# Keys' high and low parts written to the other half of the partitions by ACT copies in place of DMAs, in both mixers of a two-layer encoder step

## The chip, the cores and the metric

The kernel runs on one core of a Trainium2 chip. The engines are named as in the profile: PE is TensorE (PEld its weight loads), DVE VectorE, ACT ScalarE, POOL GpSimd, SP SyncE. PE multiplies, DVE and ACT do elementwise work; SP and POOL issue nearly all DMAs, each from a queue of its own that is worked off in order. The metric is the device time of one execution in microseconds (us), lower is better.

## The reference

One inference step over 1024 prompt frames and 8 running streams with 16 new frames each, so T = 1152 tokens of width 1024. Each of two layers is a mixer and an MLP, with RMS norms ahead. The two mixers, cut to what the change touches:

```python
def stick_breaking(q, k, v, q_pos, k_pos):          # layer 0: 8 heads of 64, beside a convolution
    z = jnp.einsum('bqhd,bkhd->bhqk', q, k).astype(jnp.float32) * (HEAD_DIM ** -0.5)
    mask = k_pos[None, :] < q_pos[:, None]
    log_keep = jnp.where(mask, jax.nn.log_sigmoid(-z), 0.0)
    between = lax.cumsum(log_keep, axis=3, reverse=True) - log_keep
    w = jnp.where(mask, jnp.exp(jax.nn.log_sigmoid(z) + between), 0.0)
    return jnp.einsum('bhqk,bkhd->bqhd', w.astype(v.dtype), v)

def band_attention(q, k, v, q_pos, k_pos, rel_bias):   # layer 1: 16 heads of 64
    s = jnp.einsum('bqhd,bkhd->bhqk', q, k).astype(jnp.float32) * (HEAD_DIM ** -0.5)
    rel = jnp.clip(q_pos[:, None] - k_pos[None, :], -REL_CLIP, REL_CLIP) + REL_CLIP
    s = s + rel_bias[:, rel].astype(jnp.float32)
    ...
    p = jax.nn.softmax(jnp.where(mask, s, -jnp.inf), axis=-1)
    return jnp.einsum('bhqk,bkhd->bqhd', p.astype(v.dtype), v)
```

In layer 1 a query sees its own chunk of 64 frames and the 8 chunks before it. The mixer's output is multiplied by an output matrix and added to the residual stream.

## The kernel before, in words

Products are taken in float32 by way of float32r, a format with fewer mantissa bits: a number is split into a high part (its float32r rounding, an ACT copy, line 185) and a low part (the rest, a DVE subtraction, line 186), and products of the parts are summed.

**Pairs of heads.** Both mixers go over pairs of heads: `mixer0` four (times 60 to 600 us), `mixer1` eight (1317 to 1930 us), some 70 us each in `mixer1`. A head has 64 dimensions, so a pair fills the 128 partitions: head 0 the lower half, head 1 the upper. While pair p is attended to, the projections of pair p+1 (`psc` in `mixer1`, `psp` in `mixer0`, with the split weights `hl_wc`, `hl_wi`) are worked off between its steps, into the buffers `sq`, `sk`, `sv` (queries, keys, values over 1152 tokens).

**`expand`** (line 342) then makes the operands of the scores for each head i of the pair, on 128 partitions: `qs[i]` has the scaled query's high part in the head's own half and its low part in the other half; `kd[i]` has the key's high part in both halves, `kl[i]` its low part in both halves. So one pass over 128 partitions gives (query high + query low) · key high, and a second one · key low. The profile writes these tiles as `q`, `k` and `l`. The own half of `kd` comes from ACT (line 348), that of `kl` from DVE (line 351); the other halves are copied from the own half by DMAs from POOL's queue (lines 349 and 352, 256 KB each).

**Scores and products.** PE multiplies into `z` (lines 943, 944) or `zc` (1220, 1221). In `mixer1`, DVE adds the bias and takes the maximum (1184), ACT exponentiates (`s`, 1187), DVE inverts the sum (1188) and normalises (1189); PE transposes the weights into `tpc` (457); ACT and DVE split them into `whc` and `wlc` (185, 186); PE multiplies with the values (`avc`, 469); ACT moves a half of the result (`atc`, 477), DVE adds it (`cpc`, 479) and POOL's queue stores it to `cat_d` in DRAM (363). In `mixer0` a sigmoid (`sg`, 947), a scan on DVE (928), transposes `tpa` (388), an ACT copy `wa` (390) and products `ava` (398) stand in the places of these.

**Output.** During the last pair the output product begins. `ready_chunks` loads the earlier pairs' results from `cat_d` into `cr` (1081, SP's queue) and splits them into `cat`, `part_out` loads the residual stream into `xo` (1098 in layer 0, 1100 in layer 1) and multiplies `cat` with the output weights into `psoa`. `cr` is a tile with the tag of the key buffer `sk`, and there is one such buffer, so a load of `cr` waits for whoever reads the keys last; `xo` has the tags of `sq` and `sv`, and its load waits for their last readers. `ct03k`, also on SP's queue, is the key cache of the samples.

**What sets the order.** The steps of a pair and the projections are merged by a list of costs in the program, and within that a scheduler places each instruction on its engine's queue by estimated readiness. Each engine works its queue in order. An instruction that takes another time, or another engine, can so move others on all engines.

```python
# ready_chunks
cr = pp.tile([P, T], F32, "sk", f"cr{layer}{c}")
dma(cr, cat_d[layer][c])
for g in range(NG):
    hi, lo = (x[:, c % 4, :] for x in cat_t[g][c // 4])
    split(hi, lo, cr[:, g * G:g * G + G])
```

Of the kernel before, what the change touches and what calls it, by code (L numbers as in the profile page):

```python
# [10 lines left out]
AF = mybir.ActivationFunctionType  # L11
# [8 lines left out]
TP = 1024  # L20
# [20 lines left out]
def f(ap):  # L41
    return ap.bitcast(F32)
# [82 lines left out]
def tile_trunk(ctx, tc, ins, outs):  # L125
    nc = tc.nc
    ACT = nc.scalar.activation
# [214 lines left out]
    def expand(qs, kd, kl, q, k):  # L342


        for i in range(2):
            own = slice(64 * i, 64 * i + 64)
            oth = slice(64 - 64 * i, 128 - 64 * i)
            ACT(kd[i][own], k[own, :TP], AF.Copy)
            nc.gpsimd.dma_start(kd[i][oth], kd[i][own])
            ACT(qs[i][own], q[own, :TP], AF.Copy, scale=0.125)  # L350
            tt(kl[i][own], k[own, :TP], f(kd[i][own]), ALU.subtract)
            nc.gpsimd.dma_start(kl[i][oth], kl[i][own])
            stt(qs[i][oth], q[own, :TP], 0.125, f(qs[i][own]), ALU.mult, ALU.subtract)

    class Cat:
# [301 lines left out]
    def mixer0():  # L657
        with ExitStack() as st:
# [228 lines left out]
            def expand_qk(p):  # L887
                q, k = S["sq", p], S["sk", p]
                expand(qs, kd, kl, q, k)
                S["qn"] = pp.tile([P, P], F32, "qn", f"qn0{p}")  # L890
                S["kn"] = pp.tile([P, P], F32, "kn", f"kn0{p}")
                ACT(S["qn"], q[:, TP:], AF.Copy, scale=0.125)
                ACT(S["kn"], k[:, TP:], AF.Copy)
# [222 lines left out]
    def mixer1(nx, win):  # L1116
        h, rstd = nx.h, nx.r
        with ExitStack() as st:
# [37 lines left out]
            def expand_qk(p):  # L1156
                q, k = S["sq", p], S["sk", p]
                expand(qs, kd, kl, q, k)
                S["qn"] = pp.tile([P, P], F32, "qn", f"qn1{p}")
                S["kn"] = pp.tile([P, P], F32, "kn", f"kn1{p}")  # L1160
                ACT(S["qn"], q[:, TP:], AF.Copy, scale=0.125)
                ACT(S["kn"], k[:, TP:], AF.Copy)
# [823 lines left out]
```

## Time and profile before

| | |
|---|---|
| three runs | 2727.28, 2727.0, 2727.28 us (median 2727.28) |
| the profiled execution | 2730.68 us, of which 2728.9 us from the first to the last instruction |
| granted clock of TensorE, mean | 0.993 |
| PE busy | 2662.6 us, 98% of the span |
| DVE, ACT, POOL busy | 2040.6, 1365.7, 330.5 us |
| DMA | 422.90 MB in 173203 packets |
| output product, `mixer0` and `mixer1` | from 400 us and from 1836 us on |

A row of the timeline reads: start in us, duration in us, engine, line, operation, what is written from what, shape, how many in a row, and in brackets how long the engine stood idle before it and what ended that. "128x512" is partitions by elements. A window's row reads: its ends, its length, busy time and number of instructions of PE, PEld, DVE, ACT and POOL, PE's granted clock (1 is full), the mean busy share of the DMA engines, GB/s. SPq and POOLq are the issuing queues.

### The profile page before, as it was taken

What the parts mean: (1) busy time and instruction counts of PE and PEld (TensorE: products, weight loads), DVE (VectorE), ACT (ScalarE), POOL (GpSimd) and SP (SyncE); (2) the same over time, 40 slices, a digit from 0 to 9 for tenths busy, and PEclk for the clock granted to TensorE, in tenths of its full rate; (3) what the DMA queues carried; (4) which work ended last, traced back from release to release, by engine and by line L of the source; (5) the groups of instructions that cost most, each with busy time, mean ns of one, the idle gap of its engine ahead of it and who ended that gap; (6) DMA issues with size and microseconds to landing.
All of it is one profiled execution on the core that took longest, in us unless ns stands there. A gap on an engine that the chain in (4) does not pass through costs nothing.

```text
span 2728.9 us, 50505 instructions
## 1 busy us (share of the span) xinstructions
PE 2662.6 (98%) x19362; PEld 2553.8 (94%) x19362; DVE 2040.6 (75%) x4105; ACT 1365.7 (50%) x2854; POOL 330.5 (12%) x599
## 2 busy tenths in 40 slices
PE   8999998999999999999999999998999999999998
PEld 8888886899999999999999999997999999999998
DVE  7999996787777755768577777778787777647577
ACT  5344456755555543445355555555455555534344
POOL 1000111131111100000011111110321111100001
PEclk9999999999999999999999999999999999999999
DMA  4344447443333486335444444446543334674344
GB/s 159 104 128 149 146 141 241 171 145 141 140 138 138 151 290 224 108 113 178 145 141 139 129 139 141 137 127 218 181 140 138 143 141 147 233 254 135 96 125 146
DMA packets 173203, 422.90 MB, mean 155 GB/s; under 512 B 25968, under 2 KB 53808, under 8 KB 170912
## 3 DMA queue, kind: packets, MB, share of 16 engines
q1 hardware_dynamic: 135696, 288.38, 32.6%
q0 software_dynamic: 37120, 131.27, 13.9%
q8 instruction: 152, 2.49, 0.4%
q14 instruction: 91, 0.75, 0.1%
q10 hardware_dynamic: 144, 0.02, 0.0%
HBM read 289.60 MB, written 117.34 MB: 149 GB/s over the span
## 4 chain that ended last, share of the span: by engine, by line
PE 84%; DVE 7%; ACT 3%; issue 3%; DMA 3%; POOL 0%; SPq 0%; DVEq 0%; ACTq 0%; POOLq 0%
PE pd L1705 26%; PE um L1480 25%; PE psc L225 10%; PE psp L225 4%; PE avc L469 2%; PE tpc L457 2%; PE psoa L225 2%; PE f L225 1%; PE zs L570 1%; PE zc L1220 1%; PE ava L398 1%; DVE y L737 1%; PE so L604 1%; PE psg L225 1%; PE psa L225 1%
## 5 line engine op out<-in xcount | busy, mean ns | idle before, releaser
L225 PE MATMUL psc<-h,hl_wc 128*128 128x384 f32 x1728 | 327.1, 339 | 0.0
L225 PEld LDWEIGHTS psc<-h,hl_wc 128*128 128x128 f32 x1728 | 296.8, 188 | 13.3 <-issue 10.9
L1480 PE MATMUL um<-sl,hl_m 128*128 128x288 f32 x1548 | 240.8, 296 | 0.0
L1480 PEld LDWEIGHTS um<-sl,hl_m 128*128 128x128 f32 x1548 | 218.2, 189 | 0.0
L1705 PE MATMUL pd<-tm,hl_wd 128*128 128x288 f32 x1584 | 214.7, 294 | 0.0
L1705 PEld LDWEIGHTS pd<-tm,hl_wd 128*128 128x128 f32 x1584 | 211.3, 189 | 0.0
L737 DVE SCALAR_TENSOR_TENSOR y<-u,dw,y 128x1024 f32<-128x1024 f32 (+1 forms) x232 | 177.5, 805 | 0.7
L1487 ACT ACTIVATE hdm<-hdm 128x288 f32<-128x288 f32 x192 | 84.7, 442 | 156.4 <-DVE hdm L1486 154.8
L225 PE MATMUL psp<-h,hl_wi 128*128 128x384 f32 x864 | 162.5, 340 | 0.0
L186 DVE TENSOR_TENSOR tm<-xr,tm 128x576 fp32r<-128x576 f32 (+1 forms) x120 | 85.7, 715 | 94.8 <-ACT tm L185 94.6
L225 PEld LDWEIGHTS psp<-h,hl_wi 128*128 128x128 f32 x864 | 148.4, 188 | 6.2 <-issue 5.1
L185 ACT ACTIVATE tm<-xr 128x576 fp32r<-128x576 f32 (+1 forms) x120 | 77.6, 647 | 94.7 <-PE pd L1705 75.9
L1480 PE MATMUL um<-sl,hl 128*128 128x288 f32 x756 | 119.1, 296 | 0.0
L1187 ACT ACTIVATE s<-s,mxc 128x640 f32<-128x640 f32 (+4 forms) x128 | 88.8, 694 | 60.2 <-DVE mxc L1184 58.6
L1705 PE MATMUL pd<-th,hl_wd 128*128 128x288 f32 x792 | 113.9, 297 | 3.8 <-DVE th L186 3.7
L1705 PEld LDWEIGHTS pd<-th,hl_wd 128*128 128x128 f32 x792 | 108.7, 191 | 4.5 <-DVE th L186 4.2
L1705 PE MATMUL pd<-xr,hl_wd 128*128 128x288 f32 x792 | 111.9, 295 | 0.0
L1705 PEld LDWEIGHTS pd<-xr,hl_wd 128*128 128x128 f32 x792 | 107.4, 189 | 0.0
L1480 PEld LDWEIGHTS um<-sl,hl 128*128 128x128 f32 x756 | 106.4, 188 | 0.8
L1705 PE MATMUL pd<-tm,hl 128*128 128x288 f32 x768 | 104.9, 295 | 0.0
L1705 PEld LDWEIGHTS pd<-tm,hl 128*128 128x128 f32 x768 | 103.1, 188 | 0.0
L185 ACT ACTIVATE whc<-tpc 128x512 fp32r<-128x512 f32 (+1 forms) x144 | 72.5, 523 | 46.7 <-PE tpc L457 45.7
(530 smaller groups left out, 6536.8 us busy)
## 6 DMA issues: line engine op xcount, KB each, us to landing
xr<-hb_d SPq DMA_DIRECT2D x208, 288.0 KB, 2.9
xr<-in_w_up_dram SPq DMA_DIRECT2D x64, 512.0 KB, 4.0
hb_d<-hdm POOLq DMA_DIRECT2D x96, 288.0 KB, 2.4
hb_d<-t POOLq DMA_DIRECT2D x96, 288.0 KB, 2.4
wm<-in_w_down_dram SPq DMA_DIRECT2D x64, 256.0 KB, 4.1
st_wd<-in_w_down_dram SPq DMA_DIRECT2D x64, 256.0 KB, 3.5
st_wc<-in_w_in_c_dram SPq DMA_DIRECT2D x44, 256.0 KB, 2.6
xm_d<-xo POOLq DMA_DIRECT2D x16, 576.0 KB, 3.8
```

The costliest lines, as they stand in the source:

```text
L185: ACT(hi, src, AF.Copy)
L186: return tt(lo, src, f(hi), ALU.subtract)
L225: mm(ps()[:, :G], hl[:, a, at:at + P], act[g][k // 4][b][:, k % 4, :], start=n == 0, stop=n == len(todo) - 1)
L398: mm(st["av"][64 * m:64 * m + 64, o0:o0 + n], vs[:, j, i], st["w"][gi][:, c0:c0 + n], start=gi == 0, stop=gi == last)
L457: nc.tensor.transpose(tp[:, c0 + q * P:c0 + (q + 1) * P], blocks.get(j, tile_q), ident)
L469: mm(st["av"][:, o0:o0 + n], vs[:, j, i].rearrange("p a d -> p (a d)"), src[:, c0:c0 + n], start=st["done"] == 0, stop=st["done"] == nmm - 1)
L570: mm(box["z"][at // 512][own, at % 512:at % 512 + kw], qb[:, own], k[:, b * kw:b * kw + kw], start=True, stop=True)
L737: stt(src if j == CW - 1 else dst, src, wj, dst, ALU.mult, ALU.add)
L1187: ACT(s[:, :n], s[:, :n], AF.Exp, bias=mx, scale=-1.0, accum_out=tot)
L1480: mm(banks[b, n][:, :TQ], w[:, a, c * P:c * P + P], combo(key, c)[:, h, n * TQ:n * TQ + TQ], start=k < 3 and c == 0 and i == 0, stop=c == ...
L1487: ACT(y, y, AF.Relu)
L1705: mm(ps, w[:, a, m * P:m * P + P], b[:, h, (n - ns[0]) * TQ:(n - ns[0]) * TQ + TQ], start=first and s == 0, stop=j == NJ - 1 and s == 2, s ...
```

## The change

In `expand`, the two DMAs are replaced by ACT copies. The key's other half is rounded from the keys again, which gives the same high part; the low part's other half is copied from DVE's result. The key copy stands after the query's.

```diff
             ACT(kd[i][own], k[own, :TP], AF.Copy)
-            nc.gpsimd.dma_start(kd[i][oth], kd[i][own])
             ACT(qs[i][own], q[own, :TP], AF.Copy, scale=0.125)
+            ACT(kd[i][oth], k[own, :TP], AF.Copy)
             tt(kl[i][own], k[own, :TP], f(kd[i][own]), ALU.subtract)
-            nc.gpsimd.dma_start(kl[i][oth], kl[i][own])
+            ACT(kl[i][oth], f(kl[i][own]), AF.Copy)
             stt(qs[i][oth], q[own, :TP], 0.125, f(qs[i][own]), ALU.mult, ALU.subtract)
```

In the changed program the copy of the query's high part is line 349, the key copy 350, the copy of the low part 352. Twelve pairs of two heads make 24 of each. The scheduler's order changes with it, and these are the places that matter below.

SP's queue at the last pair boundary of `mixer0`, between the loads of the key cache and of the output weights:

```order
 L539 DMA ct03k_4424<-in_sb_k_dram 128x4x256
 L539 DMA ct03k_4426<-in_sb_k_dram 128x4x256
+L1098 DMA xo_4607<-in_x_dram 128x3x384
 L1081 DMA cr_4356<-cat_d_109 128x1152
-L1098 DMA xo_4607<-in_x_dram 128x3x384
 L192 DMA st_wo0a_0_5016<-in_w_out_ab_dram 128x384
 L192 DMA st_wo0a_0_5182<-in_w_out_ab_dram 128x384
```

The load of the residual stream (`xo`) moved ahead of the load of an earlier pair's result (`cr`); `cr` waits for ACT now where it waited for DVE.

ACT at the same place (`sb` belongs to the samples, `sv` are the next values, `ata` is the moved half of a product):

```order
 L947 ACTIVATE sg_4252<-z_4257 128x512
 L608 ACTIVATE sb_4280<-so_4093 128x128
 L390 ACTIVATE wa_4286<-tpa_4282 128x384
+L350 ACTIVATE k_744<-sk_3769 64x1024
 L881 ACTIVATE sv_4091<-psp_4237 128x384
-L185 ACTIVATE hl_wo0a_0_4715<-st_wo0a_0_4713 128x384
-L902 ACTIVATE ve_4489<-sv_4091 64x8 x4
+L352 ACTIVATE l_746<-l_746 64x1024
 L411 ACTIVATE ata_4320<-ava_4313,ve_3530 64x128 x2
 L390 ACTIVATE wa_4371<-tpa_4366 128x512
```

The key copy, the last reader of the key buffer now, stands behind the first `wa`.

ACT at a steady boundary of `mixer1`, where pair 6's operands are made (the boundaries from pair 1 on look alike):

```order
 L348 ACTIVATE k_14069<-sk_19255 64x1024
 L185 ACTIVATE whc_19739<-tpc_19736 128x256
-L350 ACTIVATE q_14067<-sq_18957 64x1024
+L349 ACTIVATE q_14067<-sq_18957 64x1024
+L350 ACTIVATE k_14069<-sk_19255 64x1024
 L1187 ACTIVATE s_19721,totc_19732<-s_19721,mxc_19730 128x640
 L477 ACTIVATE atc_19751<-avc_19716 64x256
+L352 ACTIVATE l_14071<-l_14071 64x1024
 L185 ACTIVATE whc_19799<-tpc_19794 128x512
 L185 ACTIVATE whc_19821<-tpc_19816 128x512
```

The key copy stands ahead of the exponential, the low part's copy ahead of the next split.

DVE at the same boundary:

```order
 L351 TENSOR_TENSOR l_14071<-sk_19255,k_14069 64x1024
+L353 SCALAR_TENSOR_TENSOR q_14067<-sq_18957,q_14067 64x1024
 L1188 RECIPROCAL totc_19732<-totc_19732 128x1
 L479 TENSOR_TENSOR cpc_19753<-avc_19716,atc_19751 64x256
 L1189 TENSOR_SCALAR s_19721<-s_19721,totc_19732 128x640
-L353 SCALAR_TENSOR_TENSOR q_14067<-sq_18957,q_14067 64x1024
 L186 TENSOR_TENSOR wlc_19800<-tpc_19794,whc_19799 128x512
```

The query's low part moved ahead of the normalisation of the weights. On PE the six transposes of these weights moved behind seven matmuls of the next pair's projection.

ACT at the boundary of pairs 6 and 7 of `mixer1`, some instructions later:

```order
 L477 ACTIVATE atc_20646<-avc_20611 64x256
+L352 ACTIVATE l_14071<-l_14071 64x1024
 L185 ACTIVATE whc_20676<-tpc_20671 128x512
 L185 ACTIVATE whc_20695<-tpc_20690 128x512
+L185 ACTIVATE cat_00_20682<-cr_20680 128x384 x3
 L185 ACTIVATE whc_20727<-tpc_20724 128x256
-L185 ACTIVATE cat_00_20682<-cr_20680 128x384 x3
+L185 ACTIVATE vs_14072<-vt_20760 128x6x64
```

The three splits of `cr` stand ahead of the last `whc` of pair 6. On PE three transposes of the values (`vt`) moved ahead of the product with that `whc`.

## The prediction

> **What bounds the kernel now.** I read first the page's busy shares and its chain by engine, then the waits of TensorE, then single stretches of the two mixers.
>
> ```profile
> PE 2662.6 (98%) x19362; PEld 2553.8 (94%) x19362; DVE 2040.6 (75%) x4105; ACT 1365.7 (50%) x2854; POOL 330.5 (12%) x599
> PE 84%; DVE 7%; ACT 3%; issue 3%; DMA 3%; POOL 0%; SPq 0%; DVEq 0%; ACTq 0%; POOLq 0%
> ```
>
> TensorE (PE) is busy for 98% of the span, ACT for half of it. So ACT has room for more work on average, and the question is only where TensorE stands waiting and whether the new copies lie ahead of what it waits for. The waits of PE (us in total, times, longest), four rows of that view:
>
> ```profile
> PE psoa L225 <- ACT cat L185: 8.0, 3, 5.7
> PE avc L469 <- ACT whc L185: 6.9, 7, 1.1
> PE tpc L457 <- DVE s L1189: 6.1, 8, 3.2
> PE avc L469 <- DVE wlc L186: 2.1, 2, 1.5
> ```
>
> All four lie in the mixers, and three stand behind ACT or behind a DVE step that an ACT exponential feeds. The windows show how little PE waits there (us of the window, then busy time of PE, PEld, DVE, ACT, POOL, then PE's granted clock, DMA share, GB/s): mixer 0, mixer 1, two slices of mixer 0's last pair boundary, and one steady pair of mixer 1.
>
> ```profile
> 60.00:600.00 540.00, 519.63 (x3691) 454.51 (x3690) 469.73 (x737) 278.86 (x616) 81.29 (x118) 0.98 0.48 153
> 1317.00:1930.00 613.00, 594.12 (x4278) 559.11 (x4277) 444.54 (x1242) 325.09 (x752) 71.36 (x163) 0.99 0.46 146
> 406.00:412.00 6.00, 1.58 (x12) 0.89 (x8) 3.50 (x7) 2.32 (x7) 2.36 (x5) 0.97 1.06 341
> 412.00:418.00 6.00, 3.40 (x18) 2.45 (x18) 2.63 (x4) 2.49 (x6) 2.14 (x4) 0.50 1.09 350
> 1567.00:1637.00 70.00, 68.44 (x509) 64.58 (x505) 51.74 (x145) 38.04 (x88) 9.05 (x21) 1.00 0.44 138
> ```
>
> PE is idle 540 − 519.63 = 20.4 us in mixer 0 and 613 − 594.12 = 18.9 us in mixer 1, and 1.56 us in a steady pair of 70. In the two slices at 406 to 418 the DMA engines are full; there PE also stands longest, and runs at half clock afterwards.
>
> **The change part by part.** Removed: 24 key and 24 residual DMAs on POOL's queue. Added: 48 ACT copies of 64x1024. Their rows, from the views of lines 348, 477, 349 and 352:
>
> ```profile
> L348 ACT ACTIVATE k<-sk x24: 1047/1057/1062, 96.4 to 1837.8; 64x1024 fp32r<-64x1024 f32 x24
> L477 ACT ACTIVATE atc<-avc x64: 379/381/387, 1366.7 to 1926.2; 64x256 f32<-64x256 f32 x64
> L349 POOL DMA_DIRECT2D k<-k x24: 517/528/544, 97.8 to 1839.1; - x24
> L352 POOL DMA_DIRECT2D l<-l x24: 509/522/537, 100.2 to 1841.9; - x24
> ```
>
> ACT gains 48 × 1.057 = 50.7 us, from 1365.7 to about 1416 us. The new copies go from one half of the partitions to the other; line 477 does this for one head of each pair and not for the other, and its minimum and maximum differ by 8 ns, so I take the price of line 348 for them. POOL loses 24 × (0.528 + 0.522) = 25 us of issuing. Neither view names any engine that waited for these DMAs, so taking them away frees no PE wait by itself, and the bytes (48 × 256 KB) matter only where DMA is full. What counts is which ACT, DVE or SP instruction comes later, place by place.
>
> *First pairs and most of mixer 0: 0.* There the copies stand in front of ACT work that PE reaches later; ACT is idle for 540 − 278.86 = 261 us of mixer 0. Were that cover gone, a copy would cost its 1.06 us. Bounds −0.5 and +1.
>
> *Five steady boundaries of mixer 1.* ACT, DVE and PE rows of one:
>
> ```profile
> 1559.03 1.06 ACT L350 ACTIVATE q<-sq 64x1024 fp32r<-64x1024 f32 x1
> 1560.12 0.83 ACT L1187 ACTIVATE s<-s,mxc 128x640 f32<-128x640 f32 x1
> 1563.18 1.09 ACT L185 ACTIVATE whc<-tpc 128x512 fp32r<-128x512 f32 x2 [1.74 <-PE tpc L457]
> ...
> 1559.68 1.22 DVE L351 TENSOR_TENSOR l<-sk,k 64x1024 fp32r<-64x1024 f32 x1
> 1562.51 1.22 DVE L353 SCALAR_TENSOR_TENSOR q<-sq,q 64x1024 fp32r<-64x1024 f32 x1
> ...
> 1562.54 0.88 PE L457 MATMUL tpc<-ident,s 128*128 128x128 f32 x6 [0.38 <-DVE s L1189]
> ```
>
> The key copy now stands ahead of the exponential at 1560.12, which ends 1.06 us later. DVE does the query residual (1.22 us) in that time instead of after the normalisation, so s is ready about 0.4 us later, not 1.06. PE has seven projection matmuls ahead of the six transposes now, which cover this. The residual copy falls into ACT's idle 1.74 us. What is left is the shorter distance from the transposes to the products of whc. I take +0.2 each, between −0.3 (the wait of 0.38 goes) and +0.7 (the copy less that wait); five make +1.0.
>
> *Seven mid-pair places of mixer 1.* Here the key copy stands ahead of a whc, the residual copy ahead of the sample's weights:
>
> ```profile
> 1604.48 0.30 ACT L1162 ACTIVATE kn<-sk 128x128 f32<-128x128 f32 x1
> 1604.68 0.59 ACT L185 ACTIVATE whc<-tpc 128x512 fp32r<-128x512 f32 x1
> 1605.53 0.68 DVE L186 TENSOR_TENSOR wlc<-tpc,whc 128x512 fp32r<-128x512 f32 x1
> 1606.75 0.40 PE L469 MATMUL avc<-wlc,vs 128*128 128x256 f32 x2
> ```
>
> The small copy kn moves behind the weights, and the key copy takes its place, so whc starts at 1604.48 + 1.06 = 1605.54 and ends near 1606.13, its residual wlc near 1606.85, and PE wants that at 1606.75. I take +0.15 each, between 0 and +0.4; seven make +1.0.
>
> *Pair 6 to 7 of mixer 1.*
>
> ```profile
> 1843.44 1.54 PE L457 MATMUL tpc<-ident,s 128*128 128x128 f32 x6 [3.25 <-DVE s L1189]
> 1848.03 0.52 PE L469 MATMUL avc<-whc,vs 128*128 128x128 f32 x2
> 1846.35 0.38 ACT L185 ACTIVATE whc<-tpc 128x256 fp32r<-128x256 f32 x1 [0.67 <-PE tpc L457]
> 1848.01 1.35 ACT L185 ACTIVATE cat<-cr 128x384 fp32r<-128x384 f32 x3 [1.28 <-DMA cr<-cat_d]
> ```
>
> PE has nothing ahead of the transposes there, so the 0.4 us of s is paid. Then ACT puts the three cat copies, which wait for a load until 1848.01, ahead of the last whc: this ends at 1848.01 + 1.35 + 0.38 = 1849.74, PE comes to it near 1848.9 (0.4 later, three transposes now ahead of it). With the load up to 0.7 us earlier, since a DMA of 256 KB beside it goes (priced below), I take +0.9 in all, between −0.5 and +2.
>
> *Last boundary of mixer 0 (pairs 2 to 3).* PE, ACT, SP and DVE rows, then the landings (KB each, us from issue):
>
> ```profile
> 414.60 0.69 PE L225 MATMUL psoa<-cat,hl_wo0a 128*128 128x384 f32 x1 [5.73 <-ACT cat L185]
> 423.34 0.44 PE L225 MATMUL psoa<-cat,hl_wo0a 128*128 128x384 f32 x1 [0.83 <-ACT cat L185]
> 414.03 1.35 ACT L185 ACTIVATE cat<-cr 128x384 fp32r<-128x384 f32 x3 [4.47 <-DMA cr<-cat_d]
> 404.11 0.51 ACT L390 ACTIVATE wa<-tpa 128x384 f32<-128x384 f32 x1
> 404.62 0.34 SPq L1081 DMA_DIRECT2D cr<-cat_d  x1
> 405.88 0.89 SPq L1098 DMA_DIRECT2D xo<-in_x_dram  x1
> 404.63 1.22 DVE L353 SCALAR_TENSOR_TENSOR q<-sq,q 64x1024 fp32r<-64x1024 f32 x1
> ...
> cr<-cat_d SPq DMA_DIRECT2D x1, 576.0 KB, 9.4
> xo<-in_x_dram SPq DMA_DIRECT2D x1, 576.0 KB, 12.8
> st_wo0a<-in_w_out_ab_dram SPq DMA_DIRECT2D x2, 192.0 KB, 11.9
> ```
>
> cr takes the key's buffer. Its last reader was the DVE residual, ended at 404.6; now it is the ACT key copy, which follows the wa copy and so ends near 404.11 + 0.51 + 1.06 = 405.7, and on SP's queue xo (which waits for the query's residual, 404.63 + 1.22 = 405.85) comes first. With xo's 0.89 of issuing ahead of it, cr is issued near 406.8 instead of 404.62. It landed at 404.62 + 9.4 = 414.0, and xo at 405.88 + 12.8 = 418.7, 4.7 us later: if the queue delivers in order, cr takes xo's place. The two 256 KB DMAs that go would at 341 to 350 GB/s have taken 0.75 us each, so cr lands near 417.2 to 418, 3.3 to 4 us later. PE's queue stands at its product for that long, since what follows it is in order. Of this about 1.0 comes back at 423.34 (0.83 there, 0.15 right behind), since the second cr is less pressed by then. I take +2.9. Lower bound: cr lands only 2.2 later less 1.5 of relief, and gets 0.98 back, so about 0; upper, the full 4.7 with nothing back.
>
> The rule that decides between them is in the Trainium skill, "DMA: Bandwidth & Descriptors", section "Queues, rings and completion order": each DMA engine takes the descriptors of one issuing queue in the order of its ring, and alternates between queues packet by packet. By that rule cr does stand behind xo's bytes, and by it the sum would keep the +2.9; were it wrong and the engines shared evenly among all open transfers, the sum would be 2.9 lower. The landings at 414.0, 418.7 and 408.71 + 11.9 = 420.6 for cr, xo and the weights are in the order of issue, which agrees with the rule but doesn't prove it.
>
> Sum: 1.0 + 1.0 + 0.9 + 2.9 = **+5.8 us**. The profiled execution took 2730.68 us (span 2728.9), which makes 2736.5 after; the median of the three runs is 2727.28, 3.4 below it, which gives 2733.1.
>
> **Rivals.** *No order on SP's queue, or the relief pays for the swap* (+2.9, 2730.2): cr lands near 414.5. For it: four DMAs of each pair go, and at 406 to 418 the DMA share is 1.06 and 1.09. Against: the order of landings above.
>
> *The chains of mixer 1 are tighter than read* (+12, 2739): whc, wlc and products follow one another with waits up to 1.1 and 1.5 us in the list; if every boundary pays 0.7, every mid-pair 0.4, pair 7 its 2 and mixer 0 its 3.7, that is 3.5 + 2.8 + 2 + 3.7. Against: ACT is busy only 38.04 of 70 us in such a pair.
>
> *Faster* (−6, 2721): the wait of 5.73 at 414.60 goes. It decides itself there: cr would have to land before 409, that is with 4.4 us instead of 9.4. For it: 0.5 MB of DMA leaves just this stretch and POOL's queue has two issues less ahead of the stores. Against: 0.5 MB at 350 GB/s is 1.5 us, not 5, and cr is issued later.
>
> **How the numbers follow.** A change below 0.2%, 5.45 us, can hardly be told from none here. The forecast's own case (+3 to +9) gets 0.58, of which a little more than half, 0.33, lies above +5.45; the rival of no order 0.21 (nearly all within 0.2%); the tight chains 0.13; faster 0.08. So slower 0.46, same 0.46, faster 0.08. Time 2733.1; the range goes from 2727.5, the low end of the second case, to 2739.5, the third case.
>
> **What would show it.** L350 and L352 of the new kernel at 1.05 to 1.07 us, 24 each, and ACT at 1416; POOL at 305. The wait of psoa for cat near 9 us in place of 5.73, with cr landing after xo; if cr lands ahead of xo, that step is wrong. The PE busy time of a steady pair stays 68.4 and the pair gets 0.2 to 0.5 longer; equal or shorter pairs would make the 2 us of mixer 1 wrong. At pair 7 a new wait of avc for whc of 0.5 to 0.9. The sum fails most easily if mixer 0's wait doesn't move, or if a wait appears that I placed nowhere.

## The result, and the profile after

The changed kernel takes 2735.3 us (median of 13 runs), the kernel before 2727.0: 1.0031 times, interval [1.0023, 1.0039], so 8.3 us slower. The forecast was +5.8. The sum came near, but for other reasons than were given: of its four terms mixer 0 was too high by 2.9 us, and mixer 1 too low by 6.7.

The page's busy times of the kernel after, and its waits of PE in mixer 1 (us in total, times, longest):

```profile
PE 2666.2 (98%) x19362; PEld 2551.3 (93%) x19362; DVE 2039.9 (75%) x4105; ACT 1415.3 (52%) x2902; POOL 304.0 (11%) x551
...
PE avc L469 <- ACT whc L185: 6.9, 7, 1.1
PE tpc L457 <- DVE s L1189: 6.2, 8, 3.7
PE avc L469 <- DVE wlc L186: 3.0, 8, 1.5
PE psoa L225 <- ACT cat L185: 1.7, 1, 1.7
```

ACT and POOL have moved by about what the copies and DMAs cost (+49.6 and −26.5 us). The waits show little of the loss: avc waits for wlc 0.9 us more in all and eight times in place of two; psoa waits 1.7 us for cat, which it did in mixer 0 alone before, but 1.4 us less for cpc (2.1 before, 0.7 after); the rest is nearly as before. In the two profiled executions even the span differs by 1.6 us only (2728.9 and 2730.5), since the one of the kernel after was 6.5 us ahead when mixer 0 copied the second pair's first keys, of which more at the end. So I laid the two traces side by side at the key copies of line 348, which both have. From one such copy to the next:

| stretch of mixer 1 | before | after | difference, each | how often |
|---|---|---|---|---|
| boundary to mid-pair, steady | 44.55 | 45.93 | +1.38 | 5 |
| mid-pair to boundary, pairs 2 to 7 | 25.57 | 26.00 | +0.42 | 6 |
| the same, pair 1 | 19.28 | 20.05 | +0.77 | 1 |
| first pair; pair 1's first part | 53.90, 46.51 | 53.89, 46.53 | 0 | 1 |
| from the last boundary to the last score | 75.2 | 74.7 | −0.5 | 1 |

That is 6.9 + 2.5 + 0.8 − 0.5 = +9.7 us, and from mixer 1's first score to its last the traces show 559.8 and 569.4 us. The last row is the least sure: three profiles with the order of before in mixer 1 give 75.0 to 76.7 us there, three with the changed order 73.7 to 74.7. Mixer 0 gives nothing: from the key copy at its last boundary to the last product ava, 119.6 us before and 119.1 after. The windows of one steady pair, two rows of before and two of after:

```profile
1627.68:1672.22 44.54, 44.13 (x319) 40.90 (x318) 32.55 (x90) 23.88 (x55) 4.03 (x12) 1.00 0.45 134
1602.11:1627.68 25.57, 24.43 (x190) 23.68 (x189) 19.24 (x56) 14.16 (x34) 5.01 (x9) 1.00 0.44 143
...
1624.32:1670.25 45.93, 45.59 (x319) 41.02 (x318) 32.55 (x90) 26.04 (x57) 2.69 (x8) 1.00 0.35 119
1598.32:1624.32 26.00, 24.70 (x190) 23.74 (x189) 19.36 (x56) 16.08 (x37) 4.25 (x9) 1.00 0.36 120
```

In the first stretch PE is busy for 1.46 us longer with the same 319 matmuls at the same clock of 1.00. It isn't idle, it is busier. The groups of that stretch by shape (count, busy us, mean ns) name the matmul that brings 1.1 of the 1.46, first before, then after:

```profile
L570 PE MATMUL zs<-ct14k,qb 128*32 128x512 f32 x16 | 2.1, 604 | 0.0
...
L570 PE MATMUL zs<-ct14k,qb 128*32 128x512 f32 x16 | 3.2, 604 | 0.0
```

zs are the samples' scores: four products, each on 32 columns of the array. Sixteen records of 604 ns would be 9.7 us one after the other; before, they take 2.1 us, so they run beside one another. PE's timeline, before and then after:

```profile
1635.19 0.41 PE L469 MATMUL avc<-wlc,vs 128*128 128x256 f32 x2
1635.43 0.38 PE L457 MATMUL tpc<-ident,s 128*128 128x128 f32 x2
1635.57 0.48 PE L469 MATMUL avc<-whc,vs 128*128 128x256 f32 x2
1635.89 0.40 PE L469 MATMUL avc<-wlc,vs 128*128 128x256 f32 x2
1636.22 1.06 PE L570 MATMUL zs<-ct14k,qb 128*32 128x512 f32 x8
...
1632.03 0.38 PE L457 MATMUL tpc<-ident,s 128*128 128x128 f32 x2
1632.34 1.04 PE L570 MATMUL zs<-ct14k,qb 128*32 128x512 f32 x2
1633.32 0.50 PE L469 MATMUL avc<-wlc,vs 128*128 128x256 f32 x2
1633.66 0.40 PE L469 MATMUL avc<-whc,vs 128*128 128x256 f32 x2
1633.89 0.40 PE L469 MATMUL avc<-wlc,vs 128*128 128x256 f32 x2
1634.22 1.06 PE L570 MATMUL zs<-ct14k,qb 128*32 128x512 f32 x6
```

Before, eight records (four products) take 1.06 us. After, one product stands alone and takes 1.04, and the other three take 1.06 again. The scheduler put one zs ahead of the avc products at five boundaries. The order on PE shows this, and it was missed. The runs below in which no ACT copy of the key stands ahead of the exponential there keep the four together.

### The profile page after: what moved, and what is told of

Same layout as the page of the kernel before. It is cut to its first block, busy times and chain, and to the rows that moved or that the text cites. A ratio compares the mean times of both kernels' runs of the same rounds, so it can differ in the third digit from the quotient of the medians.

```text
span 2730.5 us, 50423 instructions
## 1 busy us (share of the span) xinstructions
PE 2666.2 (98%) x19362; PEld 2551.3 (93%) x19362; DVE 2039.9 (75%) x4105; ACT 1415.3 (52%) x2902; POOL 304.0 (11%) x551
## 4 chain that ended last, share of the span: by engine, by line
PE 84%; DVE 7%; ACT 5%; DMA 2%; issue 2%; SPq 0%; DVEq 0%; ACTq 0%
PE pd L1705 26%; PE um L1480 25%; PE psc L225 9%; PE psp L225 4%; PE avc L469 2%; PE psoa L225 2%; PE tpc L457 1%; PE zs L570 1%; PE f L225 1%; PE ava L398 1%; DVE y L737 1%; PE so L604 1%; PE tpa L388 1%; PE zc L1220 1%; PE psg L225 1%
## 5 line engine op out<-in xcount | busy, mean ns | idle before, releaser
L1480 PE MATMUL um<-sl,hl 128*128 128x288 f32 x756 | 119.1, 296 | 0.0
L186 DVE TENSOR_TENSOR wlc<-tpc,whc 128x512 fp32r<-128x512 f32 (+1 forms) x144 | 83.5, 596 | 25.6 <-ACT whc L185 22.4
```

Of the source, the lines that this page charges most:

```text
L186: return tt(lo, src, f(hi), ALU.subtract)
L1480: mm(banks[b, n][:, :TQ], w[:, a, c * P:c * P + P], combo(key, c)[:, h, n * TQ:n * TQ + TQ], start=k < 3 and c == 0 and i == 0, stop=c == ...
```

## The experiments

All were timed in five rounds; the edits are shown abridged. **Theory A:** the boundary loses by the lone zs and by the key copy's place, mid-pair loses by what stands ahead of whc, mixer 0 loses nothing. **Rival B:** the late exponential is the loss and the zs an accident of it. **Rival C:** the ACT copies slow PE's reads.

**Four zs together.** One edge for the scheduler keeps each zs behind the last traced avc product; nothing else moves but a split on DVE at each of the five places.

```diff
+    prior["avc"] = mm(st["av"][:, o0:o0 + n], ...)          # in the avc product
...
+    with tc.issue_after(prior["avc"].ins): mm(box["z"]...)   # the four zs
```

> The changed kernel with one more edge: the four sample key products zs (32 columns of the array each) stay together behind the product avc at all places, so the order of ACT, SP and POOL is that of the changed kernel, and PE's differs only at the five steady boundaries of mixer 1, where the changed kernel has one zs, then three avc products, then three zs. Theory A (a zs that stands alone takes a pass of its own of about 1.0 us): the stretch from the boundary to the middle of a steady pair falls from 45.92 us to 44.7-44.9 (before: 44.55), zs in it from 3.2 to 2.1 us, the time by 5 x 1.05 = 5 us to 2730. Rival B (the boundary is late because the key copy stands ahead of the exponential): a wait of PE takes the place of the zs, the stretch stays 45.9, 2735. Rival C (the ACT copies slow PE's reads of SBUF): nothing changes, 2735.

Measured: 2730.7 us, 1.0018 [1.0009, 1.0027]. The window of the stretch, and zs in it:

```profile
1561.36:1606.49 45.13, 44.77 (x319) 40.91 (x318) 32.49 (x90) 25.97 (x57) 2.78 (x8) 1.00 0.39 129
...
L570 PE MATMUL zs<-ct13k,qb 128*32 128x512 f32 x16 | 2.1, 604 | 0.0
```

The loss falls from 1.38 to 0.58 us a boundary; A expected a stretch of 44.7 to 44.9, so 0.15 to 0.35. B and C foresaw no change, so neither is the whole of it; the 0.58 that stay are of B's kind, and the next run shows them. The lone product costs 0.80, less than its 1.04, since it filled time in which PE waits for wlc. What remains is that wait:

```profile
1568.73 0.50 PE L469 MATMUL avc<-whc,vs 128*128 128x256 f32 x2
1569.07 0.38 PE L457 MATMUL tpc<-ident,s 128*128 128x128 f32 x2
1569.46 0.51 PE L469 MATMUL avc<-wlc,vs 128*128 128x256 f32 x2
```

The pair of transposes starts at 1569.07, and the next product 0.39 us later instead of the 0.14 of before; the following ones are spread in the same way.

**Key copy behind the exponential.** The changed kernel with one other edge:

```diff
+    prior["exp"] = ACT(s[:, :n], s[:, :n], AF.Exp, ...)
...
+    with tc.issue_after(prior["exp"].ins): ACT(kd[i][oth], k[own, :TP], AF.Copy)   # second head only
```

> The changed kernel with one other edge: the second head's key copy stands behind the last exponential on ACT and not ahead of it. At the steady boundaries of mixer 1 ACT then has exponential, key copy, atc, residual copy; PE has the six transposes four projection matmuls later than the kernel before, not seven, and the four zs stay together. If the boundary's loss (1.37 us each) all comes from the key copy's place ahead of the exponential: boundary to mid-pair 44.6 to 44.8 us (changed 45.93, zs together 45.13, before 44.55), mid-pair to boundary 26.0 as in the changed kernel, since nothing moves there; 2735.3 - 5 x 1.25 = 2729. If the two copies cost at the boundary wherever they stand: 45.1 or more, 2731 or more.

Measured: the stretch is 44.75 us, mid-pair to boundary 26.0, as expected. So 1.2 of the 1.38 come from the key copy's place ahead of the exponential, the lone zs among them, and not from the copy as such. B thus has the cause and A most of the price: the key copy ahead of the exponential is what moves the zs, and the lone zs is more than half of the loss. It also leaves C at most 0.2 us, since both ACT copies are still there.

```profile
1550.98:1595.73 44.75, 44.41 (x319) 40.96 (x318) 32.46 (x90) 25.97 (x57) 2.70 (x8) 1.00 0.39 129
```

The time was a miss: 2733.4, 1.003 [1.0021, 1.0039], where 2729 was expected. From the last boundary to the last score this kernel takes 76.8 us, where the changed one takes 74.7: the order of pair 7 moved too, and PE has two waits close together there, the second followed by 3.4 us at half clock from 1885.79 on:

```profile
1882.96 0.47 PE L469 MATMUL avc<-whc,vs 128*128 128x256 f32 x2 [1.09 <-DVE xo L1105]
1885.44 0.52 PE L469 MATMUL avc<-wlc,vs 128*128 128x256 f32 x2 [2.00 <-DVE wlc L186]
```

Most of the miss goes with the clock: its eleven executions have a granted clock of 0.9916 in the mean, the thirteen of the changed kernel 0.9934. The two at 0.994 took 2727.6 and 2726.6 us, the changed kernel's seven at 0.994 or 0.995 took 2731.3 to 2736.3, so about 6 us more, as expected. Whether the new order of pair 7 lowers the clock in the other nine isn't shown, since there is one profile of it.

**Mixer 1 alone, mixer 0 alone.** ACT copies in one mixer, DMAs in the other:

```diff
-    expand(qs, kd, kl, q, k)
+    expand(qs, kd, kl, q, k, kact, lact)     # here True (by ACT) or False (by DMA), set for each mixer
```

> ACT copies in mixer 1 alone, DMAs in mixer 0. If the loss is all in mixer 1, as the two traces say (mixer 1 +9.6 us from its first score to its last): 2736 to 2737, steady pairs of 71.9 us, the wait of psoa for cat in mixer 0 5.7 us as before with cr landing 9.4 us after its issue. As the prediction had it (mixer 1 +2.9): 2730.

> ACT copies in mixer 0 alone, DMAs in mixer 1. By the two traces mixer 0 costs nothing: 2725 to 2727, steady pairs of mixer 1 at 70.1 us, the wait of psoa for cat near 6.2 us, xo and cr both landed about 8.6 us after xo's issue. As the prediction had it: 2730 with a wait near 9 us.

Measured: 2735.3, 1.0032 [1.002, 1.0044], for mixer 1 alone, with the same stretches as the changed kernel (45.95, 26.01); 2726.1, 0.9998 [0.9989, 1.0007], for mixer 0 alone (44.56, 25.58). The loss is mixer 1's, all of it within those intervals.

**Key copy mid-pair only.** In mixer 1 the second head's key copy is a DMA again:

> The changed kernel, but in mixer 1 the key copy of the second head (at the boundary) is a DMA again; that of the first head (mid-pair) and both copies of the low part stay on ACT. PE's order at the boundary is then that of before, with the four zs together. Theory A: boundary to mid-pair 44.6 us as before, mid-pair to boundary 26.0 us as in the changed kernel (25.57 before), because the key copy stays ahead of whc there; time 2727 + 7 x 0.42 = 2730. If the residual copy at the boundary costs as well: boundary to mid-pair above 44.9. If the mid-pair loss came from the boundary's lateness: 25.6 there and 2727.

**Low part only.** In both mixers only the low part goes by ACT:

> ACT copies of the low part alone in both mixers; the key's high part goes by DMA. The order on PE in mixer 1 is that of before, with the four zs together. At the boundary the copy stands in ACT's idle time between atc and whc; mid-pair it stands ahead of the same whc as the key copy did, and starts 0.2 us later than that. If whatever stands ahead of that whc costs PE the wait: boundary to mid-pair 44.6 us as before, mid-pair to boundary 26.1 to 26.2 (25.57 before, 26.0 changed), 2727 + 7 x 0.6 = 2731 less up to 1 in mixer 0. If the key copy alone is at fault: 25.6 and 2727.

Measured: 2728.5, 1.0005 [0.9997, 1.0014], and 2727.8, 1.0004 [0.9996, 1.0013]. The windows of both, boundary to mid-pair and mid-pair to boundary:

```profile
1558.75:1603.32 44.57, 44.14 (x319) 40.91 (x318) 32.51 (x90) 24.93 (x57) 3.20 (x9) 1.00 0.42 128
1603.32:1629.33 26.01, 24.70 (x190) 23.75 (x189) 19.36 (x56) 16.07 (x37) 4.23 (x9) 1.00 0.36 121
...
1552.60:1597.15 44.55, 44.12 (x319) 40.90 (x318) 32.54 (x90) 24.91 (x56) 3.51 (x11) 1.00 0.42 128
1597.15:1623.36 26.21, 24.85 (x190) 23.79 (x189) 19.16 (x56) 15.02 (x36) 4.45 (x8) 1.00 0.41 130
```

The residual copy is free at the boundary, in ACT's idle time. Mid-pair, from pair 2 on, whichever copy stands ahead of whc costs: 0.44 us with the key copy, 0.64 with the residual copy, which starts 0.2 us later. In pair 1 only the key copy costs (20.02 us, and 19.28 with the residual copy alone, as before); why is open. Both times came out below what was expected, 2730 and 2731. With the residual copy alone six such stretches are 3.7 us, and the run shows +1.3 with an interval from −1 to +3.5; its profile is 2.5 us shorter than that of before from the last boundary to the last score, and 3.4 in mixer 0 from the last boundary to the last ava, which may make up for it.

**The swap of cr and xo.** ACT copies in mixer 0 alone, and cr's load ahead of xo's again:

```diff
+    prior["cr", c] = dma(cr, cat_d[layer][c])
...
+    with tc.issue_after(prior["cr", 0].ins): dma(xo[fc]...)
```

> ACT copies in mixer 0 alone, and the load of xo is put behind that of cr on SP's queue, so the swap of the two loads is undone while the DMAs of the keys' halves stay away. With ACT copies and xo first, three profiles of four have cr landing 8.0 to 8.6 us after its issue and PE waiting 6.2 to 6.8 us for it (the fourth 9.9 and 8.1); with DMAs and cr first (two profiles) 8.7 to 9.4 and 5.1 to 5.7, and two later waits of 0.7 to 2.4 together, which ACT copies don't show. If the queue works in order and the swap is the cost: cr lands about when xo did, 6.7 to 7.8 us after its issue, the wait falls to 4.5 to 5, the later waits stay away, 2724. If the DMA engines share their time evenly among open loads: the wait stays at 6.2 to 6.8, 2726. If the later waits had vanished because of the swap (the first product starts later): they come back, 2726.

PE's wait and the landings (KB, us from issue), the changed kernel first, then this one:

```profile
408.65 1.60 PE L225 MATMUL psoa<-cat,hl_wo0a 128*128 128x384 f32 x3 [6.21 <-ACT cat L185]
399.45 0.37 SPq L1098 DMA_DIRECT2D xo<-in_x_dram  x1
400.04 0.38 SPq L1081 DMA_DIRECT2D cr<-cat_d  x1
xo<-in_x_dram SPq DMA_DIRECT2D x1, 576.0 KB, 6.7
cr<-cat_d SPq DMA_DIRECT2D x1, 576.0 KB, 8.0
...
410.22 0.69 PE L225 MATMUL psoa<-cat,hl_wo0a 128*128 128x384 f32 x1 [4.48 <-ACT cat L185]
433.57 2.97 PE L225 MATMUL psoa<-cat,hl_wo0a 128*128 128x384 f32 x15 [1.13 <-ACT cat L185]
cr<-cat_d SPq DMA_DIRECT2D x1, 576.0 KB, 7.2
xo<-in_x_dram SPq DMA_DIRECT2D x1, 576.0 KB, 9.9
```

In all profiles the two loads land in the order of their issue, 1.6 to 4.7 us apart, and the order decides PE's first wait: 4.5 and 4.9 with cr first and no DMAs of the halves, 6.2 to 8.1 with xo first. But a later wait of 1.1 comes back with cr first, which the expectation of 2724 had staying away, so of the gain 0.6 to 2.5 is left in waits; 2724.8 us, 0.9997 [0.9988, 1.0005], which the time can't tell from the 0.9998 with xo first. The swap therefore cost PE 1.3 to 3.6 us at the first wait and saved it the later ones: all waits of psoa for cat in mixer 0 add up to 6.1 and 8.2 us in the two profiles with DMAs and cr first, and to 6.2, 6.4, 6.7, 6.8 and 8.1 in five with ACT copies and xo first. The waits are not all of it: from the key copy at the last boundary to the last ava the two profiles with ACT copies and cr first take 116.7 and 116.8 us, the five with xo first 118.3 to 121.1.

**What the runs leave of the change.** ACT copies in mixer 0 with cr first; in mixer 1 only the second head's low part.

> What the runs leave of the change: ACT copies in mixer 0 with cr's load first, in mixer 1 only the low part of the second head (at the boundary) by ACT. PE's and SP's order is that of the run with cr first. Steady pairs 70.1 us as before, the wait of psoa for cat as there; 2724 to 2725, faster than both kernels by 2 to 3 and by 10 us, if the copy in ACT's idle time is free; 2727 if it costs 0.4 us each of the seven times.

Measured: 2723.4, 0.999 [0.9981, 0.9999]. The steady pairs are as before (44.56 and 25.58). By the medians it is 12 us faster than the changed kernel; against the kernel before it is ahead by 2 to 3 us, at the edge of what the runs can tell.

## Why the prediction was right or wrong

- *ACT +50.7 us, POOL −25 us, copies at 1.05 to 1.06 us in either half:* right (1415.3, 304.0 us). First pairs at 0: right.
- *Five steady boundaries at +0.2:* mis-sized by a factor of seven, +1.38 measured. The prediction's own sign was a PE busy time of a steady pair that stays at 68.4 us and a pair longer by 0.2 to 0.5; it was 68.6 and is 70.3, and the pair is 1.8 longer. The term had two holes. The transposes' shift was taken as covered because seven projection matmuls stand ahead of them; those were taken away from behind, where they had covered wlc, and that distance was priced at 0.2 and cost 0.58. And PE's order was read as a sum of durations: the zs that moved alone was seen as a shift of work, not as work that runs a second time without company (0.80).
- *Seven mid-pair places at +0.15:* the mechanism was right, the size was off. +0.42 in six and +0.77 in pair 1, 3.3 in place of 1.0. wlc is the one that comes late, as expected; but PE loses more than it waits, as the rows of the kernel after show:

```profile
1601.90 0.60 ACT L185 ACTIVATE whc<-tpc 128x512 fp32r<-128x512 f32 x1
1602.54 0.69 DVE L186 TENSOR_TENSOR wlc<-tpc,whc 128x512 fp32r<-128x512 f32 x1 [0.58 <-ACT whc L185]
1603.28 0.51 PE L469 MATMUL avc<-wlc,vs 128*128 128x256 f32 x2 [0.16 <-DVE wlc L186]
```

  The wait is written as 0.16, yet the product starts 0.64 us after the one ahead of it, where it was 0.32, and itself takes 0.51 for 0.40. A product that follows another without a pause starts before that one's end; after a pause this overlap is lost, so this short wait cost 0.43 us, nearly three times what the row says.
- *Pair 6 to 7 at +0.9:* wrong, −0.5. The transposes' longest wait did grow from 3.2 to 3.7 as foreseen, but the new wait of avc for whc behind the cat copies didn't come. The load of cr was issued at the same place as before, 3.65 us behind the boundary's key copy, and landed after 4.84 us where it had taken 6.56; the relief had been put at no more than 0.7 (4.7 to 5.2 in the six profiles with an ACT copy of the low part there and the same place of issue, 6.6 to 7.4 in the three with both DMAs). So the cat copies start 8.5 us behind the key copy, where they had started 10.2 behind it, and the whc after them is in time:

```profile
1848.35 1.35 ACT L185 ACTIVATE cat<-cr 128x384 fp32r<-128x384 f32 x3 [0.16 <-DMA cr<-cat_d]
1849.60 0.36 ACT L185 ACTIVATE whc<-tpc 128x256 fp32r<-128x256 f32 x1
```
- *Mixer 0 at +2.9:* wrong, 0. cr is issued behind xo and lands behind it, as said, but 0.5 to 2.4 us later, counted from the key copy of line 348, and not 3.3 to 4, and more of it comes back than the 1.0 that was granted (three waits before, one after: the last, 1.44 us at 439.91, was left out of the term). That the queue delivers in order agrees with the landings; that cr lands at xo's old time less the bytes' 0.7 to 1.5 us doesn't. The relief by the removed DMAs was priced too low by the bytes: with cr first in both, the two loads have landed 12.6 and 14.1 us after the first issue with the DMAs and 10.3 and 10.7 without them (two profiles each), and 8.6 in the changed kernel, where xo is first.
- *The rivals:* the tight chains of mixer 1 were the nearest to the truth, though not by the waits that they named.

The sum of 5.8 was therefore near 8.3 by luck: mixer 1 was too low by 6.7 us and mixer 0 too high by 2.9.

## What to carry to other kernels

When an edit lets a scheduler move matmuls that use a part of the array's columns, look in the order for groups that ran side by side and now stand apart: the work counts twice, no wait shows it, and only busy time at an equal count does. A matmul moved ahead to fill a gap is taken away from somewhere; ask what it covered there. To find a loss of 1 us a round between two traces, measure from one instruction that both have to its next occurrence, before the waits are read.

## What the runs showed of the hardware that was not expected

The first pair of mixer 0 has the same wait in all ten profiles, 2.9 us for vt, and the granted clock of the six microseconds behind it was 0.50 in three, 0.75 in three and 1.00 in four, with the same kernel code up to there in several of them. Rows of before and after:

```profile
115.37 2.15 PE L913 MATMUL vt<-ident,sv 128*128 128x128 f32 x9 [2.88 <-ACT sv L904]
115.00:121.00 6.00, 5.63 (x30) 3.59 (x31) 4.02 (x6) 2.67 (x8) 0.00 (x0) 0.50 0.21 68
...
111.29 1.18 PE L913 MATMUL vt<-ident,sv 128*128 128x128 f32 x9 [2.87 <-ACT sv L904]
110.80:116.80 6.00, 5.51 (x46) 4.22 (x47) 5.78 (x8) 3.38 (x9) 0.39 (x1) 1.00 0.41 118
```

Nine transposes take 2.15 us in the one and 1.18 in the other, and the pair 2.4 us more. With the code alike, among the seven kernels with ACT copies of the keys in mixer 0, the first keys of the second pair are copied 96.6 to 96.7 us after the second keys of the first where this clock was 1.00, 98.1 where it was 0.75, and 99.3 where it was 0.50.

The traces' clock records show why it is so by chance. In each of the ten profiles every stretch of half clock begins on a grid of 3.41 us and lasts one, two or three of its steps (3.41, 6.83, 10.24 us; the first and the last stretch, cut off by the ends of the program, apart). At this wait the clock fell in the six profiles in which a grid point lay 2.0 to 2.5 us into the wait, for two steps at 2.0 to 2.1 and for one at 2.5, and not in the four in which it lay 1.1 to 1.8 us into it. One step of the run with ACT copies in mixer 1 alone, with the one ahead of it and the one behind:

```profile
110.80:114.20 3.40, 1.01 (x6) 0.69 (x4) 3.40 (x4) 0.00 (x0) 0.00 (x0) 1.00 0.50 178
114.30:117.65 3.35, 2.95 (x17) 1.98 (x17) 2.87 (x4) 1.74 (x5) 0.00 (x0) 0.50 0.00 0
117.80:121.00 3.20, 3.20 (x28) 2.71 (x25) 2.21 (x4) 1.85 (x4) 0.00 (x0) 1.00 0.61 175
```

The Trainium skill, "TensorE: Matmul & The Clock Gate", section "Part 1: The HAM clock gate (the "warmup" mystery)", says that the clock falls after at least one idle window of about 3.4 us and that the windows run freely. The length and the free run agree with these traces. That a whole window must be idle doesn't: here PE was busy for 1.01 us of the step ahead of the fall, and a wait of 2.9 us is shorter than a step.

The 4.1 us by which the kernel after was ahead at mixer 0's first key copy already are for the most part of the same kind: the profile of before has two such steps of half clock up to there, at 29.29 and 53.18 us, and that of after none. This clock is one source of the scatter of single runs (2723 to 2731 us for one kernel), and why two spans of one profile each say little about 8 us.
